# HGRN2 mix in three steps a group in place of six: levels in pairs, keys one step ahead, final transposes one group behind

## The chip, the cores and the metric

The kernel runs on one core of one Trainium2 chip. The metric is the device time of one execution in microseconds (us), and a kernel's time is the median of several executions. The engines, by the names that the profile uses, are PE (TensorE, with PEld for its weight loads), DVE (VectorE), ACT (ScalarE), POOL (GpSimd) and SP (SyncE, which issues the DMAs).

## The reference, cut to what matters

One step of a two-layer encoder: 1,024 prompt frames and eight streams of 16 frames, so nine chunks of 128 rows. Each layer multiplies the normalised frames by one input matrix, runs four kinds of recurrence (four heads or head pairs each) over the result, and multiplies by an output matrix. The change is in the fourth kind, HGRN2. Its recurrence has a decay for every channel:

```python
def hgrn_block(s_prev, xs):
    q, k, v, lf = xs
    b = jnp.cumsum(lf, axis=2)
    diff = b[:, :, :, None, :] - b[:, :, None, :, :]
    w = jnp.exp(jnp.where(causal_tril(l)[:, :, None], diff, -jnp.inf))
    s = jnp.einsum("bhtk,bhsk,bhtsk->bhts", q, k, w)
    o = jnp.einsum("bhts,bhsv->bhtv", s, v) + jnp.einsum("bhtk,bhkv->bhtv", q * jnp.exp(b), s_prev)
    s_new = jnp.exp(bl)[..., None] * s_prev + jnp.einsum("bhsk,bhsv->bhkv", k * jnp.exp(bl[:, :, None, :] - b), v)
    return s_new, o
...
    ho = head_rms(from_blocks(ho)) * h_norm_w.astype(f32).reshape(H_HEADS, H_HD)
    out_h = ho.reshape(bsz, t, GROUP_WIDTH) * jax.nn.silu(hg)
```

## The kernel before

**Units.** A layer is ten units in a fixed order: h0, r0, s0, m0, h1, r1, s1, m1, h2, h3 (h is an HGRN2 head, r retention, s Mamba-2, m mLSTM). A unit has a projection, which is most of PE's work, and a mix, its recurrence. `merge` (L1754 to 1782) writes both into one stream for each engine: the mix of one unit goes between the projection matmuls of the next. So the mixes of h0 and h1 lie in the projections of r0 and r1, that of h2 in h3's, and that of h3 in the first half of the output projection; in two layers there are eight HGRN2 mixes.

**The projection.** It works in fp32r as three products, hi by hi, lo by hi and hi by lo. In a token-major run ("tm", L425 to L427, 256 columns wide) and in a feature-major run ("fm", L404 to L406, 384 wide) it yields after every three matmuls. r0 and r1 have 216 yields, h3 has 120 (72 tm, then 48 fm), the first half of the output projection has 288.

**Steps.** A mix is a generator. After projection yield i, `merge` runs mix steps as long as j * yields * pace < i * steps, j being the steps already run. `steps` is a number that the unit gives. The pace is 1, but 0.9 from h2 to h3, where besides the last six steps of h2 are carried into the merge behind h3. What a step hands to `after(1, ...)` is issued at the start of the next step, ahead of that step's own work. All engines run in order, so this text order is the order in each queue, and every tile of PSUM comes from one ring of eight banks.

**One HGRN2 mix.** The nine chunks are three groups of three. The causal product with per-channel decay is cut into a base of 32x32 blocks and five levels (li = 0 to 4, blocks of 64, 32, 16, 8 and 4). For each group there are:

- `level` (L1486): two subtractions on DVE and an exp on ACT; a step later one multiply on POOL and one on DVE, all 192 columns wide.
- `prep` (L1505): decayed queries Q and keys K (exp on ACT, subtract on DVE), a step later the multiplies, K's on DVE and Q's on POOL.
- `base` (L1526): 12 matmuls of 32x32 (L1534).
- `pick` (L1540): the score blocks of one level, three matmuls of 64x64 or six of 32x32 (L1564), 12 of 32x16 (L1552); copies a step later, and after level 4 `diag` (L1574), four copies on DVE.
- `keys` (L1580): K transposed on PE (L1584). `state` (L1596): K transposed times values on PE (L1603), then `update` (L1613) on DVE. `out` (L1635): scores times values, queries times state (L1642, L1644).
- `post` (L1648): squares on ACT and the root mean square; a step later `scale` (L1662) on DVE. `fin` (L1667): three transposes on PE (L1671), evacuated on ACT.

The part of the step loop that sets the order (L1689 to 1716): a group takes six steps, li = -1 (base and prep) and li = 0 to 4 (a pick each). Each step also begins the level three picks ahead (LOOK = 3). At li = 4 that is level 2 of the next group, and at li = -1 of the next group it is level 2 again; the second overwrites the first. Around the six steps, keys are at li = 1, the state at li = 3, and of the group before, the outputs are at li = 0 and 1, post at 2 and fin at 4.

**What else DVE, ACT and POOL do there.** They split the weights into hi and lo, evacuate the projection, and for h3's fm run a forget-gate chain for each group (`ev_qf`, L1402: L526, L1415, L1417, L1424, then `fours`, L1435). In the output projection ACT and DVE split the mix read back from memory (mxh, mxl).

Of the kernel before, what the change touches and what calls it, by code (L numbers as in the profile page):

```python
# [51 lines left out]
NG = 3  # L52
CLAMP = -43.0
NLEV = 5
# [66 lines left out]
class Kernel:  # L121
# [1276 lines left out]
    def unit_h(self, l, h):  # L1398
# [52 lines left out]
        if h == 0:  # L1451
            gt = self.p_lay.tile([128, NCH, 16], F32, name="gt")
# [22 lines left out]
        def mix():  # L1475
            hw = self.vB[:, 40 + 4 * l + h:40 + 4 * l + h + 1]
            stt = {}
            LOOK = 3
# [6 lines left out]

            def level(W, g, li):  # L1486
                hs = 64 >> li
                w = G3 if (g < 2 or hs <= 8) else 256
                X = self.f()
                W["X"][li] = X, w  # L1490
                xv = lambda a: a[:, 0:w].rearrange("p (n e t) -> p n e t", e=2, t=hs)
                ref = xv(b[g])[:, :, 0, hs - 1:hs].to_broadcast([128, w // (2 * hs), hs])
                self.tt(xv(X)[:, :, 0], ref, xv(b[g])[:, :, 0], ALU.subtract)
                self.tt(xv(X)[:, :, 1], xv(b[g])[:, :, 1], ref, ALU.subtract)
                self.act(X[:, 0:w], X[:, 0:w], AF.Exp)

                def mults():
                    self.tt(xv(X)[:, :, 0], xv(X)[:, :, 0], xv(k[g])[:, :, 0], ALU.mult, "p")
                    self.tt(xv(X)[:, :, 1], xv(X)[:, :, 1], xv(q[g])[:, :, 1], ALU.mult)

                self.after(1, mults)

            sv = lambda a, n=3: a[:, 0:128 * n].rearrange("p (c t) -> p c t", t=128)

            def prep(g, W):  # L1505

                Q = self.f()
                K = self.f()
                np_ = 3 if g < 2 else 2
                e = bl.pop(g)  # L1510
                W.update(Q=Q, K=K, eL=e)
                self.act(Q, b[g], AF.Exp)
                self.tt(sv(K, np_), e[:, 0:np_][:, :, None].to_broadcast([128, np_, 128]), sv(b[g], np_), ALU.subtract)
                if g == 2:
                    s8 = lambda a: a[:, 256:384].rearrange("p (n t) -> p n t", t=16)
                    self.tt(s8(K), e[:, 2:10][:, :, None].to_broadcast([128, 8, 16]), s8(b[g]), ALU.subtract)
                self.act(K, K, AF.Exp)
                self.act(e[:, 0:3 if g < 2 else 10], e[:, 0:3 if g < 2 else 10], AF.Exp)

                def mults():  # L1520
                    self.tt(K, K, k[g], ALU.mult)
                    self.tt(Q, Q, q[g], ALU.mult, "p")

                self.after(1, mults)

            def base(g, W):  # L1526


                sc = self.ps("sc")
                for c in range(3):  # L1530
                    for j in range(4):
                        rs = slice(32 * j, 32 * j + 32)
                        ts = slice(128 * c + 32 * j, 128 * c + 32 * j + 32)
                        nc.tensor.matmul(sc[rs, 32 * c:32 * c + 32], k[g][:, ts], q[g][:, ts], start=True, stop=True)  # L1534
                W["ST"], W["D"] = ST, D = self.f(), self.t(96)
                nc.gpsimd.memset(ST, 0.0)
                nc.gpsimd.memset(D, 0.0)
                self.after(1, lambda: nc.vector.copy_predicated(D, self.lev[:, LEVW - 96:], sc[:, 0:96]))

            def pick(g, W, li):  # L1540
                hs = 64 >> li
                x, w = W["X"].pop(li)
                n = w // 128
                sc = self.ps("sc")
                half = lambda a: a.rearrange("p (n e t) -> p n e t", e=2, t=hs)[:, :, 1]
                if li >= 2:
                    D = W["D"]
                    for c in range(n):
                        for j in range(4):
                            rs = slice(32 * j, 32 * j + 32)  # L1550
                            xt = x[:, 128 * c + 32 * j:128 * c + 32 * j + 32]
                            nc.tensor.matmul(sc[rs, 16 * c:16 * c + 16].rearrange("p (n t) -> p n t", t=hs), xt, half(xt),  # L1552
                                             start=True, stop=True)
                    cp = lambda a: a.rearrange("p (n t) -> p n t", t=hs)
                    mk = self.lev[:, 48 * (li - 2):48 * (li - 2) + 16 * n]
                    self.after(1, lambda: nc.vector.copy_predicated(half(D[:, 0:32 * n]), cp(mk), cp(sc[:, 0:16 * n])))
                    if li == NLEV - 1:
                        self.after(1, lambda: diag(W))
                    return
                for c in range(n):  # L1560
                    for j in range(64 // hs):
                        rs = slice(64 * j, 64 * j + hs)
                        xt = x[:, 128 * c + 64 * j:128 * c + 64 * j + 2 * hs]
                        nc.tensor.matmul(sc[rs, hs * c:hs * c + hs], xt[:, 0:hs], xt[:, hs:2 * hs], start=True, stop=True)  # L1564

                def put():
                    for j in range(64 // hs):
                        rs = slice(64 * j, 64 * j + hs)
                        self.copy(sv(W["ST"][rs], n)[:, :, 64 * j + hs:64 * j + 2 * hs],
                                  sc[rs, 0:hs * n].rearrange("p (c t) -> p c t", t=hs), BIG[li])  # L1570

                self.after(1, put)
# [23 lines left out]
            def state(g, W):  # L1596

                n = 3 if g < 2 else 2
                tr = self.ps("tr")
                for cc in range(n):  # L1600
                    j, i = divmod(3 * g + cc, 2)
                    cs = slice(128 * cc, 128 * cc + 128)
                    nc.tensor.matmul(tr[:, cs], W["KT"][:, cs], v[j][:, i, 0], start=True, stop=True)  # L1603
                S = self.f()

                def update():
                    for cc in range(n):
                        c = 3 * g + cc
                        cs = slice(128 * cc, 128 * cc + 128)
                        if c == 0:  # L1610
                            self.copy(S[:, cs], tr[:, cs], "v")
                        else:
                            nc.vector.scalar_tensor_tensor(out=S[:, cs], in0=SS[c], scalar=W["eL"][:, cc:cc + 1], in1=tr[:, cs],  # L1613
                                                           op0=ALU.mult, op1=ALU.add)
                        SS[c + 1] = S[:, cs]
                        if c == 7:
                            self.dma(T["o_p_h"][l, h], S[:, cs])

                self.after(1, update)

            def state_s(W, jj):
                tr = self.ps("tr")
# [57 lines left out]
            Ws = [{"X": {}} for _ in range(NG)]  # L1680
# [3 lines left out]
            level(Ws[0], 0, 0)  # L1684
            yield
            level(Ws[0], 0, 1)
            for _ in range(2 if h < 2 else 2):
                yield
            for g in range(NG):  # L1689
                W = Ws[g]  # L1690
                for li in range(-1, NLEV):
                    if li < 0:
                        base(g, W)
                        prep(g, W)
                    else:
                        pick(g, W, li)
                    if li + LOOK < NLEV:
                        level(W, g, li + LOOK)
                    elif g + 1 < NG:
                        level(Ws[g + 1], g + 1, li + LOOK - NLEV)  # L1700
                    if li == 1:
                        keys(g, W)
                    if li == 3:
                        state(g, W)
                        if g == 1:
                            load_states()
                    if g > 0:
                        V = Ws[g - 1]
                        for cc in {0: (0,), 1: (1, 2)}.get(li, ()):
                            out(g - 1, V, cc)  # L1710
                        if li == 2:
                            post(g - 1, V)
                        if li == 4:
                            fin(g - 1, V)
                            Ws[g - 1] = None
                    yield
            W = Ws[2]
            yield
            yield
            out(2, W, 0)  # L1720
            out(2, W, 1)
            out(2, W, 2)
            yield
            post(2, W)
            yield
            state_s(W, 0)
            yield
            state_s(W, 1)
# [2 lines left out]
            fin(2, W)  # L1731
            yield

        return dict(runs=[("tm", ev_vg), ("fm", ev_qf)], mix=mix, steps=31 if h < 2 else 29, gate=(lambda: self.gate_prep(l, gt)) if h == 0 else None)


    def mix_load(self, l, half, g):
# [263 lines left out]
```

## Time and profile before

| | before |
|---|---|
| median of 3 runs | 2383.02 us (2382.79 to 2383.59) |
| profiled execution, device time | 2383.27 us |
| its span in the profile | 2381.4 us |
| PE busy in the span | 2315.6 us (97%) |
| DVE, ACT, POOL busy | 1367.5, 1082.4, 935.8 us |
| mean granted clock of PE | 0.994 of full |

The profile is that of one execution. PE is busy for all but 65.8 us of the span. The busy share of an engine is a mean over all stages; how engines stand to each other in an HGRN2 mix is seen only in a stretch that holds one. In the timeline a row merges neighbouring instructions of a line, under the shape of the first, and a matmul of fp32 values is recorded as two passes, so 12 instructions of 32x16 stand as x24.

### The profile page before, as it was taken

Reading aid. Unit: us, or ns where it says so; the run is one execution under the profiler, and the core shown is the slowest. Engines: PE = TensorE matmul, PEld = TensorE weight load, DVE = VectorE, ACT = ScalarE, POOL = GpSimd, SP = SyncE. Lnnn points to the kernel's source line nnn. Section 1 sums busy time; section 2 is a strip of 40 time slices with the busy share of each in tenths; the row PEclk is TensorE's granted clock in tenths of the full one; section 3 lists DMA queues with packets and bytes.
Section 4 is the critical chain, followed back from the end, with each engine's and each line's share of the span. In section 5 each row is a group of like instructions: output and inputs, shape, how many; then the busy total and the mean of one; then the engine's idle time right before and its main releaser. Section 6 shows DMA issues by size and latency. Waiting matters only on the chain.

```text
span 2381.4 us, 51682 instructions
## 1 busy us (share of the span) xinstructions
PE 2315.6 (97%) x20104; PEld 2251.8 (95%) x20104; DVE 1367.5 (57%) x3426; ACT 1082.4 (45%) x2881; POOL 935.8 (39%) x1117
## 2 busy tenths in 40 slices
PE   7999999999999998999999999999999999899998
PEld 7899999999999998999998999999899999888998
DVE  4756753774765377553258476537747555766532
ACT  6344563433555345424354445634344653453333
POOL 2442344353334335434316333433633452344341
PEclk9999999999999999999999999999999999999999
DMA  5111232221123222546411212322111323225462
GB/s 153 37 47 53 79 90 78 66 61 53 50 84 96 62 73 66 171 126 207 136 49 34 62 55 85 87 70 74 49 54 52 105 72 83 50 86 163 146 189 96
DMA packets 280048, 205.24 MB, mean 86 GB/s; under 512 B 56788, under 2 KB 272236, under 8 KB 279804
## 3 DMA queue, kind: packets, MB, share of 16 engines
q1 hardware_dynamic: 279484, 201.85, 29.9%
q8 instruction: 159, 2.61, 0.5%
q14 instruction: 85, 0.70, 0.1%
q0 software_dynamic: 320, 0.09, 0.0%
HBM read 149.58 MB, written 52.29 MB: 85 GB/s over the span
## 4 chain that ended last, share of the span: by engine, by line
PE 84%; DVE 8%; ACT 4%; DMA 1%; issue 1%; SPq 1%; POOL 1%; ACTq 0%; DVEq 0%; POOLq 0%
PE w L425 16%; PE w L427 16%; PE w L426 16%; PE w L404 6%; PE w L405 6%; PE w L406 6%; DVE f L212 3%; ACT f L215 2%; PE w L1289 1%; DVE c L212 1%; DMA c<-mixd 1%; PE w L1642 1%; PE w L1603 1%; PE w L1552 1%; PE w L1043 1%
## 5 line engine op out<-in xcount | busy, mean ns | idle before, releaser
L425 PE MATMUL w<-hi,hnh 128*128 128x256 f32 (+1 forms) x2592 | 773.3, 298 | 0.0
L427 PE MATMUL w<-hi,hnl 128*128 128x256 f32 (+1 forms) x2592 | 730.1, 282 | 1.6 <-DVE hnl L492 1.4
L426 PE MATMUL w<-lo,hnh 128*128 128x256 f32 (+1 forms) x2592 | 729.3, 281 | 0.0
L425 PEld LDWEIGHTS w<-hi,hnh 128*128 128x128 f32 x2592 | 490.6, 189 | 5.7 <-issue 0.8
L426 PEld LDWEIGHTS w<-lo,hnh 128*128 128x128 f32 x2592 | 490.9, 189 | 2.9
L427 PEld LDWEIGHTS w<-hi,hnl 128*128 128x128 f32 x2592 | 490.3, 189 | 2.2 <-DVE hnl L492 2.0
L215 ACT ACTIVATE f<-f 128x384 f32<-128x384 f32 (+1 forms) x460 | 236.3, 516 | 427.7 <-DVE f L212 263.5
L215 ACT ACTIVATE c<-c 128x512 f32<-128x512 f32 (+3 forms) x398 | 211.3, 534 | 286.3 <-DVE c L526 202.2
L212 POOL TENSOR_TENSOR f<-f,f 128x384 f32<-128x384 f32 (+2 forms) x268 | 225.6, 849 | 290.7 <-ACT f L215 216.3
L404 PE MATMUL w<-hnh,hi 128*128 128x384 f32 x960 | 338.8, 353 | 0.0
L425 PE MATMUL w<-hi,mxh 128*128 128x256 f32 x1152 | 329.4, 286 | 0.0
L427 PE MATMUL w<-hi,mxl 128*128 128x256 f32 x1152 | 325.2, 282 | 0.2 <-POOL mxl L212 0.2
L426 PE MATMUL w<-lo,mxh 128*128 128x256 f32 x1152 | 324.9, 282 | 0.0
L406 PE MATMUL w<-hnh,lo 128*128 128x384 f32 x960 | 324.6, 338 | 0.0
L405 PE MATMUL w<-hnl,hi 128*128 128x384 f32 x960 | 324.6, 338 | 0.0
L212 POOL TENSOR_TENSOR lo<-raw,hi 128x512 fp32r<-128x512 f32 x148 | 196.4, 1327 | 304.3 <-ACT hi L202 278.3
L212 POOL TENSOR_TENSOR c<-c,c 128x512 f32<-128x512 f32 (+2 forms) x144 | 160.3, 1122 | 273.3 <-ACT c L215 169.5
L425 PEld LDWEIGHTS w<-hi,mxh 128*128 128x128 f32 x1152 | 219.0, 190 | 1.4 <-issue 0.6
L427 PEld LDWEIGHTS w<-hi,mxl 128*128 128x128 f32 x1152 | 219.0, 190 | 0.8 <-POOL mxl L212 0.8
L426 PEld LDWEIGHTS w<-lo,mxh 128*128 128x128 f32 x1152 | 218.2, 189 | 0.0
L212 DVE TENSOR_TENSOR lo<-raw,hi 128x512 fp32r<-128x512 f32 x140 | 114.8, 820 | 149.9 <-ACT hi L202 149.7
L404 PEld LDWEIGHTS w<-hnh,hi 128*128 128x128 f32 x960 | 181.5, 189 | 3.0 <-issue 1.8
(295 smaller groups left out, 3876.8 us busy)
## 6 DMA issues: line engine op xcount, KB each, us to landing
raw<-in_w_in SPq DMA_DIRECT2D x224, 128.0 KB
raw<-in_w_in SPq DMA_DIRECT2D x112, 256.0 KB
c<-mixd SPq DMA_DIRECT2D x96, 192.0 KB
raw<-in_w_out SPq DMA_DIRECT2D x64, 256.0 KB
mixd<-c SPq DMA_DIRECT2D x48, 256.0 KB
xd<-c SPq DMA_DIRECT2D x48, 256.0 KB
c<-xd SPq DMA_DIRECT2D x48, 256.0 KB
c<-sscr SPq DMA_DIRECT2D x36, 256.0 KB
```

Of the source, the lines that this page charges most:

```text
L212: (self.nc.vector if e == "v" else self.nc.gpsimd).tensor_tensor(out=out, in0=a, in1=b, op=op)
L215: self.nc.scalar.activation(out=out, in_=in_, func=func, scale=scale, bias=bias, **k)
L404: nc.tensor.matmul(o, hi[:, k, ms], xhi[:, k, :], start=(k == 0), stop=False)
L405: nc.tensor.matmul(o, hi[:, k, ms], xlo[:, k, :], start=False, stop=False)
L406: nc.tensor.matmul(o, lo[:, k, ms], xhi[:, k, :], start=False, stop=(k == KT - 1))
L425: nc.tensor.matmul(o, xhi[:, k, ts], hi[:, k, :w], start=(k == 0), stop=False)
L426: nc.tensor.matmul(o, xhi[:, k, ts], lo[:, k, :w], start=False, stop=False)
L427: nc.tensor.matmul(o, xlo[:, k, ts], hi[:, k, :w], start=False, stop=(k == KT - 1))
L1043: nc.tensor.matmul(po[h], w[:, h], v[j][:, i, h], start=(c in (0, 8)), stop=(c < 8))
L1289: nc.tensor.matmul(po[:, 64 * h:64 * h + 64], pt[:, h], x_[:, 64 * h:64 * h + 64], start=True, stop=True)
L1552: nc.tensor.matmul(sc[rs, 16 * c:16 * c + 16].rearrange("p (n t) -> p n t", t=hs), xt, half(xt), start=True, stop=True)
L1603: nc.tensor.matmul(tr[:, cs], W["KT"][:, cs], v[j][:, i, 0], start=True, stop=True)
```

## The change

The group loop is written out with three steps, called A, B and C here:

- A: base, pick 0, levels 3 and 4 begun, the state of the group before, post of the group two before.
- B: picks 1 and 2, keys, level 0 of the next group begun.
- C: picks 3 and 4, the three outputs of the group before, fin of the group two before, levels 1 and 2 and prep of the next group begun (in the last group, the loads of the streams' states instead).

Each level, and with prep the decayed keys and queries, is begun two steps ahead of the matmul that takes it. Level 2 of a next group is begun once. The state's update is issued in the same step as its matmuls, not a step later. The prelude begins three levels and prep; the tail brings the last state, post and fin. `steps` goes from 31 to 21 (h0, h1) and from 29 to 19 (h2, h3).

```diff
@@ state
-                self.after(1, update)
+                update()
@@ mix, the group loop
-            for _ in range(2 if h < 2 else 2):
+            level(Ws[0], 0, 2)
+            prep(0, Ws[0])
+            yield
+            yield
+            for g in range(NG):
+                W, V = Ws[g], Ws[g - 1]
+                base(g, W)
+                pick(g, W, 0)
+                level(W, g, 3)
+                level(W, g, 4)
+                if g > 0:
+                    state(g - 1, V)
+                if g > 1:
+                    post(g - 2, Ws[g - 2])
                 yield
-            for g in range(NG):
-                W = Ws[g]
-                for li in range(-1, NLEV):
-                    if li < 0:
-                        base(g, W)
-                        prep(g, W)
-                    else:
-                        pick(g, W, li)
-                    if li + LOOK < NLEV:
-                        level(W, g, li + LOOK)
-                    elif g + 1 < NG:
-                        level(Ws[g + 1], g + 1, li + LOOK - NLEV)
...
+                pick(g, W, 1)
+                pick(g, W, 2)
+                keys(g, W)
+                if g + 1 < NG:
+                    level(Ws[g + 1], g + 1, 0)
+                yield
+                pick(g, W, 3)
+                pick(g, W, 4)
+                if g > 0:
+                    for cc in range(3):
+                        out(g - 1, V, cc)
+                if g > 1:
+                    fin(g - 2, Ws[g - 2])
+                if g + 1 < NG:
+                    level(Ws[g + 1], g + 1, 1)
+                    level(Ws[g + 1], g + 1, 2)
+                    prep(g + 1, Ws[g + 1])
+                else:
+                    load_states()
+                yield
             W = Ws[2]
...
+            state(2, W)
+            post(1, Ws[1])
+            yield
+            yield
+            for cc in range(3):
+                out(2, W, cc)
             yield
             post(2, W)
-            yield
+            fin(1, Ws[1])
             state_s(W, 0)
             yield
             state_s(W, 1)
@@
-        return dict(runs=[("tm", ev_vg), ("fm", ev_qf)], mix=mix, steps=31 if h < 2 else 29, gate=(lambda: self.gate_prep(l, gt)) if h == 0 else None)
+        return dict(runs=[("tm", ev_vg), ("fm", ev_qf)], mix=mix, steps=21 if h < 2 else 19, gate=(lambda: self.gate_prep(l, gt)) if h == 0 else None)
```

The order on PE in group 1 of h1, before: pick 1 between two projection matmuls, with the keys' transposes and two outputs of group 0 (w is a PSUM tile, f and c are tiles in SBUF, hi and lo weights, hnh and hnl the input).

```order
3285 L427 MATMUL w_6577<-hi_6088,hnl_159 128x256
3286 L1564 MATMUL w_6590<-f_6395 32x32 x6
3287 L1584 MATMUL w_6601<-cst,f_6512 128x128 x3
3288 L1642 MATMUL w_6561<-c_5182,f_6210 128x128
3289 L1644 MATMUL w_6561<-f_6403,f_6214 128x128
3290 L1642 MATMUL w_6561<-c_5302,f_6210 128x128
3291 L1644 MATMUL w_6561<-f_6403,f_6214 128x128
3292 L425 MATMUL w_6577<-hi_6088,hnh_158 128x256
```

Of the change, step B of the same group.

```order
3289 L427 MATMUL w_6560<-hi_6076,hnl_159 128x256
3290 L1564 MATMUL w_6582<-f_6444 32x32 x6
3291 L1552 MATMUL w_6589<-f_6448 32x16 x12
3292 L1584 MATMUL w_6602<-cst,f_6453 128x128 x3
3293 L425 MATMUL w_6560<-hi_6076,hnh_158 128x256
```

Pick 2, which stood 21 projection matmuls later, now follows pick 1 directly, and the outputs have gone to step C. Counted over the program, 176 stretches of HGRN2 matmuls stand between projection matmuls before and 112 now; those with score blocks (bases and picks) are 144 before and 72 now, of which 24 hold a base and a pick 0, and 48 two picks.

The order on DVE before, at the state of group 1 of h1: a copy of pick 3 and half of a level, then `update` (L1613), issued a step after its matmuls.

```order
703 L212 TENSOR_TENSOR f_6707<-f_6026 128x4x32 x2
704 L1556 COPY_PREDICATED t_6508<-lev,w_6694 128x6x8
705 L212 TENSOR_TENSOR f_6707<-f_6707,f_5999 128x4x32
706 L1613 SCALAR_TENSOR_TENSOR f_6715<-f_6403,bl_5947,w_6711 128x128
707 L1613 SCALAR_TENSOR_TENSOR f_6715<-f_6715,bl_5947,w_6711 128x128 x2
```

Of the change, steps A (to the second L1613 row) and the start of B, in group 1 of h1.

```order
679 L205 COPY f_6280<-t_6281 32x3x32 x4
680 L212 TENSOR_TENSOR f_6444<-f_6444,f_5819 128x6x32
681 L212 TENSOR_TENSOR f_6448<-f_6448,f_5819 128x12x16
682 L212 TENSOR_TENSOR f_6453<-f_6453,f_5925 128x384
683 L212 TENSOR_TENSOR f_6521<-f_5923 128x24x8 x2
684 L212 TENSOR_TENSOR f_6525<-f_5923 128x48x4 x2
685 L205 COPY f_6533<-w_6529 128x128
686 L1613 SCALAR_TENSOR_TENSOR f_6533<-f_6533,bl_5746,w_6529 128x128 x2
687 L1538 COPY_PREDICATED t_6514<-lev,w_6500 128x96
688 L205 COPY f_6513<-w_6517 64x3x64
689 L212 TENSOR_TENSOR f_6521<-f_6521,f_5819 128x24x8
690 L212 TENSOR_TENSOR f_6525<-f_6525,f_5819 128x48x4
```

The multiplies for levels 1 and 2 and the keys, four subtractions and the update of group 0 (685, 686) now stand in one step, the update ahead of the multiplies (689, 690) that picks 3 and 4 of step C take.

## Rows read from the trace of the kernel before

**Rows 1.** Page, part 1: busy us, share of the span and instructions of each engine

```profile
PE 2315.6 (97%) x20104; PEld 2251.8 (95%) x20104; DVE 1367.5 (57%) x3426; ACT 1082.4 (45%) x2881; POOL 935.8 (39%) x1117
```

**Rows 2.** Waits of PE: line and what it waited for, us in total, times, longest

```profile
PE w L1671 <- DVE f L1662: 12.5, 4, 4.1
PE w L1584 <- DVE f L212: 12.0, 8, 2.9
PE w L1564 <- POOL f L212: 6.9, 4, 3.2
PE w L1603 <- ACT f L202: 4.4, 7, 0.7
PE w L1552 <- POOL f L212: 4.3, 5, 1.2
```

**Rows 3.** Windows of 3.4 us: busy us of each engine (instructions), granted clock, DMA

```profile
513.50:516.90 3.40, 3.40 (x17) 3.40 (x18) 2.87 (x9) 1.05 (x2) 0.77 (x1) 0.51 0.02 5
2162.20:2165.60 3.40, 3.31 (x15) 3.16 (x16) 1.49 (x5) 0.58 (x1) 3.40 (x4) 0.50 0.72 231
```

**Rows 4.** Timeline of PE round one pick: start, us, instruction, [idle before]

```profile
111.42 0.28 PE L426 MATMUL w<-lo,hnh 128*128 128x256 f32 x1
111.54 0.28 PE L427 MATMUL w<-hi,hnl 128*128 128x256 f32 x1
111.75 0.38 PE L1552 MATMUL w<-f 128*32 128x16 f32 x24
112.06 0.38 PE L425 MATMUL w<-hi,hnh 128*128 128x256 f32 x1
112.28 0.28 PE L426 MATMUL w<-lo,hnh 128*128 128x256 f32 x1
```

**Rows 5.** Groups of PE by line and shape: count, busy us, mean ns, idle before

```profile
L1552 PE MATMUL w<-f 128*32 128x16 f32 x1664 | 27.1, 187 | 4.4 <-POOL f L212 4.3
```

**Rows 6.** Timeline, GpSimd then PE, at level 0 of group 0 (h2 mix)

```profile
889.87 2.74 POOL L212 TENSOR_TENSOR f<-f,f 128x384 f32<-128x384 f32 x3 [1.73 <-ACT f L215]
892.66 0.56 PE L1564 MATMUL w<-f 128*64 128x64 f32 x6 [1.97 <-POOL f L212]
```

**Rows 7.** Timeline, DVE then PE, at the key transposes of unit h0

```profile
107.23 2.51 DVE L212 TENSOR_TENSOR f<-f,f 128x384 f32<-128x384 f32 x2
108.81 0.41 PE L1584 MATMUL w<-cst,f 128*128 128x128 f32 x2 [2.41 <-DVE f L212]
```

**Rows 8.** Timeline, DVE then PE, at the final transposes beside a forget-gate chain

```profile
945.30 0.86 DVE L1662 SCALAR_TENSOR_TENSOR f<-w,s,c 128x128 f32<-128x128 f32 x3
945.79 0.75 PE L1671 MATMUL w<-cst,f 128*128 128x128 f32 x3 [2.24 <-DVE f L1662]
```

**Rows 9.** Timeline, PE, DVE, PE: outputs and final transposes in the output projection

```profile
961.90 0.39 PE L1642 MATMUL w<-c,f 128*128 128x128 f32 x2
975.30 0.36 DVE L1448 TENSOR_SCALAR f<-t 128x384 f32<-128x384 f32 x1
982.84 0.85 DVE L1662 SCALAR_TENSOR_TENSOR f<-w,s,c 128x128 f32<-128x128 f32 x3
983.23 0.85 PE L1671 MATMUL w<-cst,f 128*128 128x128 f32 x3 [3.02 <-DVE f L1662]
```

**Rows 10.** Groups of DVE by line and shape: count, busy us, mean ns, idle before

```profile
L212 DVE TENSOR_TENSOR f<-f 128x192 f32<-128x192 f32 x208 | 114.6, 590 | 0.0
L212 DVE TENSOR_TENSOR f<-f,f 128x192 f32<-128x192 f32 x104 | 51.9, 499 | 21.1 <-ACT f L215 20.7
L212 DVE TENSOR_TENSOR f<-f,f 128x384 f32<-128x384 f32 x24 | 16.8, 698 | 0.0
L205 DVE COPY f<-t 32x96 f32<-32x96 f32 x96 | 23.5, 244 | 1.8
L1613 DVE SCALAR_TENSOR_TENSOR f<-f,bl,w 128x128 f32<-128x128 f32 x56 | 19.4, 346 | 3.3 <-PE w L1603 1.9
```

**Rows 11.** Windows, columns as in group 3, of a mix stretch of unit h0

```profile
113.50:129.00 15.50, 14.25 (x180) 13.09 (x179) 14.51 (x39) 6.09 (x17) 9.37 (x15) 1.00 0.09 20
```

More of the change, by code (lines that the diff above doesn't have):

```diff
@@ L1686, in mix @@
             level(Ws[0], 0, 1)
-            for _ in range(2 if h < 2 else 2):
-                yield
-            for g in range(NG):
-                W = Ws[g]
-                for li in range(-1, NLEV):
-                    if li < 0:
-                        base(g, W)
-                        prep(g, W)
-                    else:
-                        pick(g, W, li)
-                    if li + LOOK < NLEV:
-                        level(W, g, li + LOOK)
-                    elif g + 1 < NG:
-                        level(Ws[g + 1], g + 1, li + LOOK - NLEV)
[L1701 to L1716, printed above, removed]
@@ L1717, in mix @@
-            W = Ws[2]
+            level(Ws[0], 0, 2)
+            prep(0, Ws[0])
             yield
             yield
-            out(2, W, 0)
-            out(2, W, 1)
-            out(2, W, 2)
+            for g in range(NG):
[29 more added lines that the diff above has]
+                yield
@@ L1723, in mix @@
+            W = Ws[2]
+            state(2, W)
[4 more added lines that the diff above has]
+                out(2, W, cc)
             yield
             post(2, W)
-            yield
+            fin(1, Ws[1])
             state_s(W, 0)
```

## The prediction

> **What bounds the kernel now.** I read the page's first part, the waits of PE, the windows of low granted clock, then the timeline at each kind of wait. PE bounds the whole: busy 2315.6 us, and no other engine has two thirds of that [rows 1]. So an edit in the mix is worth what it takes from PE's stream, its waits, or its time at the low clock. The waits that belong to HGRN2 are five kinds, 12.5 + 12.0 + 6.9 + 4.4 + 4.3 = 40.1 us [rows 2]: the final transposes wait for the scale (L1662), the key transposes for the multiply on DVE, the picks for the multiply on POOL, the state matmuls for the evacuated keys. Each is an operand begun one or two short steps before PE takes it. Besides, seven stretches of 3.4 us stand at half the granted clock, 1.2 in place of 2.4 GHz; the first and the last are shown [rows 3], and the last begins as a wait of 4.1 us for the scale ends [rows 2, 3].
>
> The sum below is made against the profiled execution, 2383.27 us, which lies 0.25 us above the median of 2383.02.
>
> **The change part by part.**
>
> *Fewer entries into the array.* Projection matmuls start 0.12 us apart; from the last one ahead of a pick to the second one behind it are 111.54 to 112.28 = 0.74 us, where two spacings would be 0.24 [rows 4]. The extra is 0.50. The pick's merged row is 0.38 long and one pass in it 0.187 [rows 4, 5], so the 24 passes take 0.38 - 0.19 = 0.19 from first start to last, and the remaining 0.31 is entering and leaving. Two picks behind each other should pay that once. There are 72 stretches with score blocks fewer: 48 are two picks on 32 rows, 48 * 0.31 = 14.9 us. The other 24 pair a base on 32-row tiles with a 64x64 pick, which no row shows; I take half, 24 * 0.155 = 3.7. Together **18.6 us**. Bounds: 0 (each block drains by itself) to 72 * 0.31 = 22.3; no loss, as the same matmuls run between the same neighbours.
>
> The pick in rows 4 shows that going between a projection matmul and a 32-row pick costs 0.31 us. The Trainium skill, TensorEngine Tiling (Array Packing), Key Properties, says: "Mode switching requires drain: Changing tiling mode (not just tile) drains the TensorE." The row agrees; by the rule the pair of base and 64x64 pick would drain between its halves too and save nothing, the sum of this part would be 14.9, and no run here shows such a pair.
>
> *The waits that go.* The key multiply and the levels now start a longer and earlier step ahead. A step of h0 and h1 is 216/21 = 10.3 yields of three matmuls, 10.3 * 0.36 = 3.7 us of projection, where it was 216/31 = 7.0 and 2.5; and keys and levels now have one full step between their multiplies' issue and the matmul. The wait of 2.41 us was for DVE's pair of multiplies of 2.51 us issued in the step just ahead [rows 7], the one of 1.97 for three on POOL, 2.74 us [rows 6]. At the same durations 3.7 us and the mix on top cover both. The 12.0 and 6.9 and 4.3 us go almost wholly, as do the 4.4 at the state matmuls, since keys are evacuated a step or more before.
>
> *The final transposes.* In h2 they stand beside h3's forget-gate chains. Group 0's (two waits, 2.24 us in the one shown [rows 8]) get their scale a step earlier and lie a whole chain later: gone. The other two, the larger ones, I expect to stay. Of group 1, post is now the last step ahead of the output projection, so the scale is issued in its first step, on DVE right behind the third forget-gate chain. That chain's last instruction starts at 975.30 and is 0.36 long, and the scale's first third takes some 0.34 [rows 9, 10], so operands are there at about 976.0. PE begins the output projection at 961.9 [rows 9] and comes to the transposes 24 yields later, 24 * 0.36 + 0.9 for the outputs ahead = 9.5 us: 971.4. So PE would wait **about 5 us** in each of the two layers, 10 us, where it waited for group 2's scale (3.02 [rows 9], the other 4.1). Group 2's transposes stand at yield 58, past all that.
>
> *The waits that come.* `update` is now issued in the step of its own matmuls, ahead of levels 3 and 4's multiplies on DVE. What is queued behind it are these multiplies, the base's copy and pick 0's. Step A has on DVE: four diagonal copies 0.98, two level multiplies 1.00, the keys' multiply 0.70, four subtractions 2.36, three updates 1.04, in all 6.1 us [rows 10], against some 4.7 of PE (3.7 and about 1.0 of base, pick and state). So DVE reaches the update last, some 5 us after the step's start, when PE's state matmuls are past: it doesn't wait for PE. But it ends step A 1.4 us late. Step B has two multiplies 1.00, two subtractions 1.18 and a scale of three, some 1.0; step C a multiply 0.50, four subtractions 2.36 and the keys' 0.70; with small copies about 3.8 each [rows 10], against 4.7 and more of PE, so the lateness is made up within a group. In group 2 the keys' PSUM bank is released by that update; I allow 0.6 us in each of eight mixes, 5 us. For the denser h2, 2 us in each layer, 4 us.
>
> Left of the 40.1 us are 10 + 5 + 4 = 19; **21 us** go. Bounds: 33 (only 7 left) and 5 (35 left).
>
> *The low clock.* A stretch of 3.4 us at half costs 1.7 us. I expect the two behind the output projection's wait to stay and one elsewhere: seven become three, 4 * 1.7 = **6.8 us**; bounds 2 and 10.
>
> *Work taken off other engines.* The second issue of level 2 goes: 16 levels of two subtractions and a multiply on DVE, 16 * (2 * 0.59 + 0.50) = 26.9 us [rows 10], with an exp on ACT and a multiply on POOL. None of it is on PE; it is what lets DVE carry shorter groups, and I count it at nothing itself.
>
> *Moved with them.* The two loads of the streams' states go from group 1 to the last step of group 2, behind the mix fetches on SP's queue. They have two steps of 3.7 us before the outputs take them in h0 and h1. I count nothing; were they late by one step, 3.7 * 8 = 30 us would come back, part of the rivals below.
>
> Sum: 2383.3 - 18.6 - 21 - 6.8 = **2337 us**. With all good ends 2383.3 - 22.3 - 33 - 10 = 2318, with all bad ones 2383.3 - 0 - 5 - 2 = 2376; together in one direction they are unlikely, and I take 2314 to 2362 as the main case's own range.
>
> **The rivals.**
>
> *DVE becomes the bound of the groups.* Before, a stretch of h0's mix had DVE busy 14.51 of 15.50 us [rows 11]. A group now has about 6.1 + 3.8 + 3.8 = 13.7 us on DVE, in three steps of 4.7 to 5.4 us of PE, some 14.8; other work on DVE (clamps, splitting weights) is not in that. For it: no slack to speak of. Against it: the duplicate level is gone, and the prelude has begun three levels ahead. If the lateness of step A (1.4, with small copies 1.8 us) comes out on PE in groups 1 and 2 of eight mixes, 16 * 1.8 = 29 us: 2366.
>
> *The update stops DVE: slower.* If PE is late into step A, DVE stands at L1613 until the state matmuls have run, with the multiplies for picks 3 and 4 behind it, and PE then stands at those picks. The chain from update to pick is 1.04 + 1.00 + copies and the POOL half, about 3.5 us; in 24 groups 84 us, so 2337 + 84 = 2421. It makes the change slower than before from 46/24 = 1.9 us a group on. Against it: pick and multiply are a step of 3.7 us apart, and before DVE waited 1.9 us in all for L1603 [rows 10].
>
> *Nothing comes of it.* Each block drains by itself and the waits only move: 2383 - 5 = 2378 at the least saving, within reach of 2383.
>
> *The pairs of unlike tiles drain.* Then the 3.7 us of base and pick 0 don't come: 2341. Rows 4 shows a drain where the whole array meets 32-row tiles, which speaks for it as much as against.
>
> **How the numbers follow.** Main case with either end for the unlike pairs 0.73 (of which 0.3 is the 2341 variant, inside its range); DVE as the bound 0.15; update slower 0.07; nothing 0.05. About 0.2% (4.8 us) is what a measurement of this kernel can tell from no change. Faster: 0.73 + 0.15 = 0.88; same 0.05; slower 0.07. The range reaches from the main case's low end to DVE's rival at 2366, and leaves out the last two cases and the main case's tails.
>
> **What would show it.** PE's waits at the key transposes and picks should fall from 23.2 us to a few; the four waits at the final transposes should be two, of some 5 us, early in the output projection, each with a low-clock stretch behind it. A pair of picks should take, from the last projection matmul ahead to the second behind, 0.74 + 0.19 = 0.93 us. DVE's wait for L1603 should stay under a few us. The prediction is wrong if a pair takes 1.24, if PE waits at picks 3 and 4 in each group, or if DVE is busy throughout the groups with PE waiting at each key transpose.

## The result and the profile after

The changed kernel takes 2366.02 us (median of four runs, 2365.48 to 2368.27) against 2382.90 of before (four runs): a ratio of 0.9932, 95% interval 0.9915 to 0.9949. It is faster by 17 us where 46 were forecast, and its time lies at the very end of the range, where the rival with DVE as the bound stood and not the main case.

| | before | after |
|---|---|---|
| profiled execution, device time | 2383.27 us | 2365.53 us |
| its span | 2381.4 | 2363.8 |
| PE busy | 2315.6 | 2299.2 |
| span less PE busy | 65.8 | 64.6 |
| waits of PE at HGRN2's lines | 40.1 (five kinds; 1.1 more at the outputs) | 38.6 |
| time at half the granted clock, the end left out | 23.9 in 7 stretches | 34.1 in 6 |

So nearly all of the 17.6 us of span came out of PE's busy time (16.4), and the waits stayed in sum. The page's first part and the waits of PE after the change:

```profile
PE 2299.2 (97%) x20104; PEld 2247.7 (95%) x20104; DVE 1340.5 (57%) x3378; ACT 1075.9 (46%) x2865; POOL 922.5 (39%) x1101
```

```profile
PE w L1564 <- POOL f L212: 17.7, 9, 3.1
PE w L1671 <- DVE f L1662: 13.4, 2, 7.1
...
PE w L1552 <- DVE f L212: 4.1, 4, 1.7
...
PE w L1552 <- POOL f L212: 1.8, 5, 0.7
...
PE w L1584 <- DVE f L212: 1.6, 2, 0.8
```

Beside [rows 2]: the key transposes (L1584) fell from 12.0 to 1.6 us, and the state matmuls (L1603, 4.4) are gone from the list. The picks of levels 0 and 1 (L1564) rose from 6.9 to 17.7, and the final transposes (L1671) have two waits in place of four, with more in them. DVE has 48 instructions fewer, those of level 2, and 27 us less of busy time.

**The entries.** Two picks behind each other, and a base with a pick 0 (timeline of PE after: start, us, instruction):

```profile
1011.84 0.28 PE L427 MATMUL w<-hi,mxl 128*128 128x256 f32 x1
1012.05 0.60 PE L1552 MATMUL w<-f 128*32 128x16 f32 x48
1012.58 0.38 PE L425 MATMUL w<-hi,mxh 128*128 128x256 f32 x1
```

```profile
105.67 0.28 PE L427 MATMUL w<-hi,hnl 128*128 128x256 f32 x1
105.88 0.40 PE L1534 MATMUL w<-f,f 128*32 128x32 f32 x24
106.21 0.56 PE L1564 MATMUL w<-f 128*64 128x64 f32 x6
...
106.92 0.28 PE L426 MATMUL w<-lo,hnh 128*128 128x256 f32 x1
```

From the last projection matmul to the first behind it a pair of picks takes 0.74 us, where one pick took 0.52 [rows 4]: 0.22 us more for a whole second pick, whose extra alone was 0.50. The pair saves some 0.28; to the second projection matmul, at 1012.80, it takes 0.96 us, where 0.93 was forecast. A base and a pick 0 take 1.25 us to the second projection matmul, 1.01 over two spacings of 0.12; before, a base alone cost 0.75 - 0.24 = 0.51 in the same way (0.52 is the median of 24), and a 64x64 pick alone 0.92 - 0.24 = 0.68 (timeline of PE before):

```profile
98.80 0.28 PE L427 MATMUL w<-hi,hnl 128*128 128x256 f32 x1
99.01 0.40 PE L1534 MATMUL w<-f,f 128*32 128x32 f32 x24
...
99.55 0.28 PE L426 MATMUL w<-lo,hnh 128*128 128x256 f32 x1
```

```profile
500.89 0.28 PE L427 MATMUL w<-hi,hnl 128*128 128x256 f32 x1
501.10 0.56 PE L1564 MATMUL w<-f 128*64 128x64 f32 x6
...
501.81 0.28 PE L426 MATMUL w<-lo,hnh 128*128 128x256 f32 x1
```

So this pair saves 0.19 (0.52 + 0.68 - 1.01).

**The final transposes in the output projection.** ACT, DVE and PE in layer 1, after the change:

```profile
958.73 2.61 ACT L202 ACTIVATE mxh<-c 128x384 fp32r<-128x384 f32 x5 [1.89 <-DMA c<-mixd]
960.31 2.28 DVE L212 TENSOR_TENSOR mxl<-c,mxh 128x384 fp32r<-128x384 f32 x2 [0.46 <-ACT mxh L202]
962.51 0.55 DVE L526 TENSOR_SCALAR f<-w 128x384 f32<-128x384 f32 x1
...
968.87 0.36 DVE L1448 TENSOR_SCALAR f<-t 128x384 f32<-128x384 f32 x1
969.14 0.86 DVE L1662 SCALAR_TENSOR_TENSOR f<-w,s,c 128x128 f32<-128x128 f32 x3
969.54 0.99 PE L1671 MATMUL w<-cst,f 128*128 128x128 f32 x3 [7.05 <-DVE f L1662]
```

The scale starts as the third forget-gate chain ends (968.87 + 0.36), as forecast, and PE has been waiting since 962.49. The chain begins at L526, 10.7 us after the output projection's first matmul (951.78); before, it began 7.3 us after it (961.54):

```profile
968.85 0.55 DVE L526 TENSOR_SCALAR f<-w 128x384 f32<-128x384 f32 x1
```

The windows of low clock that begin inside this wait, and inside its sibling in layer 2 (columns as in rows 3):

```profile
965.66:972.49 6.83, 2.95 (x14) 2.80 (x15) 5.67 (x13) 3.46 (x8) 4.20 (x6) 0.50 0.38 119
2133.02:2143.26 10.24, 5.97 (x28) 5.82 (x29) 6.99 (x14) 5.89 (x13) 7.17 (x8) 0.50 0.37 115
```

PE was idle for about half of either (busy 2.95 of 6.83 and 5.97 of 10.24 us), so these cost well under half their length.

**Level 0 on POOL.** DVE, ACT, POOL and PE in the first mix, group 1 (the multiply of level 0 is the first of the three in the second POOL row):

```profile
118.63 0.61 DVE L212 TENSOR_TENSOR f<-f 128x192 f32<-128x192 f32 x2
119.33 0.53 ACT L215 ACTIVATE f<-f 128x384 f32<-128x384 f32 x1 [1.18 <-DVE f L212]
120.52 1.56 POOL L212 TENSOR_TENSOR c<-c,c 128x256 f32<-128x256 f32 x2 [3.04 <-DVE c L212]
...
124.91 2.00 POOL L212 TENSOR_TENSOR f<-f,f 128x192 f32<-128x192 f32 x3
125.87 0.83 PE L1564 MATMUL w<-f 128*64 128x64 f32 x6 [2.08 <-POOL f L212]
```

The exp is done at 119.86. POOL comes to the multiply at 124.91, five us later: ahead of it stand the retention unit's rotary products, which had themselves waited 3.04 us for DVE's evacuation. Four of the nine waits at L1564 look like this one, 8.4 us together, all at the 64x64 pick in r0 and r1; a fifth wait at that pick, 1.3 us, is in h3. The largest of the rest, 3.1 and 2.8 us, are at pick 1 of h2's group 0, in h3; there POOL's multiply stands behind a weight split and a gate product.

By units, as the time from one unit's first projection matmul to the next unit's, read from the trace (us; the last column is a version that the experiments led to):

| | before | after | late transposes and level 0 on DVE |
|---|---|---|---|
| r0, layers 1 and 2 | 101.33, 102.22 | 101.50, 100.75 | 97.68, 99.08 |
| r1 | 99.63, 99.35 | 96.99, 96.97 | 94.15, 94.87 |
| h3 | 78.27, 80.37 | 70.37, 72.11 | 70.01, 71.78 |
| output projection, first half | 130.14, 131.19 | 131.89, 133.62 | 127.19, 129.41 |

A row holds one HGRN2 mix, so some 2.3 us of saved entries (18.0 over eight mixes) are in each figure of the two later columns. h3 gained 16 us in both layers together, 8.4 of it waits of PE; r0 and the output projection, where the waits grew, gained 1.5 us at most or lost.

### The profile page after: what moved, and what is told of

Same layout as the page of the kernel before. It is cut to its first block, busy times and chain, and to the rows that moved or that the text cites. A ratio compares the mean times of both kernels' runs of the same rounds, so it can differ in the third digit from the quotient of the medians.

```text
span 2363.8 us, 51602 instructions
## 1 busy us (share of the span) xinstructions
PE 2299.2 (97%) x20104; PEld 2247.7 (95%) x20104; DVE 1340.5 (57%) x3378; ACT 1075.9 (46%) x2865; POOL 922.5 (39%) x1101
## 4 chain that ended last, share of the span: by engine, by line
PE 82%; DVE 8%; ACT 3%; POOL 2%; DMA 2%; issue 1%; SPq 1%; ACTq 0%; POOLq 0%; DVEq 0%
PE w L427 16%; PE w L425 16%; PE w L426 15%; PE w L404 6%; PE w L406 6%; PE w L405 6%; DVE f L212 2%; ACT f L215 2%; DMA c<-mixd 2%; POOL c L212 1%; PE w L1289 1%; DVE c L212 1%; PE w L1642 1%; PE w L489 1%; PE w L1043 1%
## 5 line engine op out<-in xcount | busy, mean ns | idle before, releaser
L427 PE MATMUL w<-hi,hnl 128*128 128x256 f32 (+1 forms) x2592 | 731.0, 282 | 1.5 <-DVE hnl L492 1.4
L427 PEld LDWEIGHTS w<-hi,hnl 128*128 128x128 f32 x2592 | 491.1, 189 | 2.1 <-DVE hnl L492 1.9
L215 ACT ACTIVATE f<-f 128x384 f32<-128x384 f32 (+1 forms) x444 | 224.2, 517 | 378.1 <-DVE f L212 193.9
L427 PE MATMUL w<-hi,mxl 128*128 128x256 f32 x1152 | 324.9, 282 | 1.0 <-POOL mxl L212 1.0
L212 POOL TENSOR_TENSOR f<-f,f 128x384 f32<-128x384 f32 (+2 forms) x252 | 212.4, 859 | 232.7 <-ACT f L215 168.8
L427 PEld LDWEIGHTS w<-hi,mxl 128*128 128x128 f32 x1152 | 218.7, 190 | 1.5 <-POOL mxl L212 1.4
L212 DVE TENSOR_TENSOR lo<-raw,hi 128x512 fp32r<-128x512 f32 x140 | 122.0, 871 | 151.6 <-ACT hi L202 151.4
L212 DVE TENSOR_TENSOR c<-c,w 128x512 f32<-128x512 f32 (+1 forms) x112 | 74.2, 665 | 199.3 <-PE w L427 158.0
```

The lines of the kernel that those rows point to most:

```text
L212: (self.nc.vector if e == "v" else self.nc.gpsimd).tensor_tensor(out=out, in0=a, in1=b, op=op)
L215: self.nc.scalar.activation(out=out, in_=in_, func=func, scale=scale, bias=bias, **k)
L427: nc.tensor.matmul(o, xlo[:, k, ts], hi[:, k, :w], start=False, stop=(k == KT - 1))
```

## The experiments

Each is the changed kernel with one edit, if nothing else is said. Ratios are against the kernel before, measured on the same chip; the changed kernel stands at 0.9932. Gains in us are differences of medians, within 2 us of what the ratios give; the intervals of two ratios together leave about 5 us to either side of such a difference.

**Blocks apart.** Each step is cut in halves, and base, pick 2 and pick 4 stand in the second half; `after` lags, `steps` and the steps carried behind h3 are doubled.

```diff
-                base(g, W)
                 pick(g, W, 0)
                 level(W, g, 3)
...
                 yield
+                base(g, W)
+                yield
                 pick(g, W, 1)
-                pick(g, W, 2)
                 keys(g, W)
...
                 yield
+                pick(g, W, 2)
+                yield
                 pick(g, W, 3)
-                pick(g, W, 4)
...
                 yield
+                pick(g, W, 4)
+                yield
```

> The changed kernel with each step cut in two halves: the first pick and all else in the first half, the second block (base, pick 2, pick 4) in the second, so a base and a pick, or two picks, no longer stand behind each other on PE; what was issued one step later is issued two halves later. Theory (each of 72 stretches costs an entry of 0.31 us more, 0.19 for the base and pick 0): 48 * 0.29 + 24 * 0.19 = 18 us more, 2384. Rival (entries cost nothing, and the 17 us gained came from waits): 2366 within 4.

Measured 2382.39 us, ratio 0.9996 (0.9986 to 1.0005): 16.4 us of the change's 17 are given back, near the 18 expected. PE's busy time is 15.7 us more than the changed kernel's 2299.2, and its idle time, 65.1 us, is the same within 0.5; the waits hardly moved (L1564 18.0 us, L1671 12.3).

```profile
PE 2314.9 (97%) x20104; PEld 2252.1 (95%) x20104; DVE 1339.3 (56%) x3378; ACT 1076.4 (45%) x2865; POOL 922.3 (39%) x1101
```

In the same way as above, as medians at the full clock and without a wait, a base alone takes 0.76 us here and a 64x64 pick 0.92; together they took 1.25 in the changed kernel, so with the two spacings (0.24) taken off once, 0.19 is saved again. Pick 1 with the keys takes 1.03 and pick 2 alone 0.74, and together they took 1.20: 0.33 saved. The gain that the change made is that of the entries.

**Transposes later.** In h2's mix `fin(1)` moves behind the streams' second state.

```diff
             post(2, W)
-            fin(1, Ws[1])
+            if h != 2:
+                fin(1, Ws[1])
             state_s(W, 0)
             yield
             state_s(W, 1)
             yield
+            if h == 2:
+                fin(1, Ws[1])
             yield
```

> Of the changed kernel (2366 us) one thing is moved: in h2's mix alone the final transposes of group 1 stand two steps later, in the step after the streams' second state. Theory (the saved entries came as forecast, and the gain was lost where PE waits at those transposes behind the third forget-gate chain, 7.05 and 6.36 us, and in the low clock that follows): the two waits go, 13.4 us, and part of the low-clock time beside them (6.8 and 10.2 us at half, worth up to 5), so 2348 to 2353 us. Rival (the forget-gate chain holds PE anyway, through group 2's transposes or the output projection's operands): the wait reappears a few us later at another line, and the time stays at 2363 to 2367.

Measured 2357.85 us, 0.9891 (0.9875 to 0.9908): 8 us gained, between theory and rival. The waits at L1671 are gone, but 5.6 us of new waits stand at the projection's own operand (PE w L427 for mxl on POOL, 1.0 to 6.6 us). PE and POOL there, layer 1:

```profile
967.58 0.38 PE L427 MATMUL w<-hi,mxl 128*128 128x256 f32 x1 [2.14 <-POOL mxl L212]
```

```profile
965.73 0.75 POOL L209 COPY bl<-f 128x2 f32<-128x2 f32 x2 [4.38 <-DVE f L1424]
966.44 1.09 POOL L212 TENSOR_TENSOR mxl<-c,mxh 128x384 fp32r<-128x384 f32 x1
```

POOL's split of the mix stands behind a tiny copy that waits for the same forget-gate chain. So the chain holds PE on a second way, and of 13.4 us of waits about 8 could be had; PE's idle time fell by 7.9 us, from 64.6 to 56.7.

**Level 0 on DVE.** One word in `level`:

```diff
-                    self.tt(xv(X)[:, :, 0], xv(X)[:, :, 0], xv(k[g])[:, :, 0], ALU.mult, "p")
+                    self.tt(xv(X)[:, :, 0], xv(X)[:, :, 0], xv(k[g])[:, :, 0], ALU.mult, "v" if li == 0 else "p")
```

> Of the changed kernel, level 0's first multiply (half of the columns) is done on DVE in place of POOL; 24 multiplies of about 0.5 us change engines. Theory (PE waits for level 0's pick, five of nine waits and about 8 of 17.7 us at L1564, because that multiply stands on POOL behind the retention unit's rotary products, which wait for DVE's evacuation): the waits at the 64x64 pick of groups 1 and 2 go, 6 to 9 us, 2357 to 2361. Rival (DVE itself is late in these steps, as it was forecast for DVE as the bound): adding 0.5 us to DVE per group lengthens the same waits, 2366 to 2375.

Measured 2357.74 us, 0.9892 (0.9877 to 0.9907): 8 us gained, as the theory had it, with more work on DVE (1345.8 us busy after 1340.5). Waits of PE:

```profile
PE w L1671 <- DVE f L1662: 14.4, 2, 7.4
...
PE w L1564 <- POOL f L212: 7.9, 4, 3.0
```

L1564 fell from 17.7 to 7.9 us (0.9 more stands under DVE), all waits at the picks from 23.6 to 15.3, and r0 and r1 became 1.7 to 3.3 us shorter in each layer. The cause of these waits was POOL's queue, not DVE.

**Update a step later.**

```diff
-                update()
+                self.after(1, update)
```

> Of the changed kernel, the state's update is issued a step after its matmuls again, as before the change. DVE now waits 23.3 us at the update for PE's state matmuls. Theory (that wait is an effect, PE stands at level 0's pick ahead of the state matmuls, and DVE has time): within 3 us of 2366. Rival (the update at the head of DVE's queue keeps the multiplies for picks 3 and 4 from running, and so causes PE's waits): 2366 less 5 to 15 us.

Measured 2373.78 us, 0.9962 (0.9947 to 0.9977): 8 us slower, which neither expected. The units r0, r1 and h3 moved by 0.7 us in all (single ones by up to 1.6 either way); the output projections lost 5.4 and 4.3. There, DVE and PE:

```profile
965.14 0.36 DVE L1448 TENSOR_SCALAR f<-t 128x384 f32<-128x384 f32 x1
965.41 0.72 DVE L1613 SCALAR_TENSOR_TENSOR f<-f,bl,w 128x128 f32<-128x128 f32 x2
```

```profile
965.81 0.79 PE L1644 MATMUL w<-f,f 128*128 128x128 f32 x2 [11.94 <-DVE f L1613]
```

The last state's update falls behind the third forget-gate chain, and the outputs wait 12 us for it (12.8 in layer 2), in place of the 7.1 and 6.4 us at the final transposes. The immediate update is what keeps it ahead of that chain.

**Update a step later in the groups only** (`update() if g == 2 else self.after(1, update)`).

> The changed kernel with the state's update a step after its matmuls in groups 0 and 1, and in the same step only for group 2 (the tail). The kernel with all updates a step later lost 8 us in the output projection alone, where the last update came behind the third forget-gate chain and PE waited 12 us for it in each layer. Theory (in the groups the place of the update decides nothing, in the tail it is worth those 8 us and more): 2364 to 2368. Rival (the update at the head of DVE's queue causes PE's waits in the groups): 2355 to 2362.

Measured 2363.92 us, 0.9917 (0.9901 to 0.9934): just between the two forecasts, and not to be told from the changed kernel. The interval alone would leave room for a gain of some us; the trace shows none in the waits: PE waits 23.3 us at the picks (23.6 in the changed kernel) and is idle for 65.0 us (64.6). DVE's wait for the state matmuls, in the changed kernel

```profile
DVE f L1613 <- PE w L1603: 23.3, 6, 5.0
```

stays at 19.6 us in four waits of 4.9. All four are at the update of group 2 in r0 and r1, the tail, where no wait of PE stands. So the update at the head of DVE's queue does no harm that shows.

**Level 2 begun twice again.** In step B, beside `level(Ws[g + 1], g + 1, 0)`, a `level(Ws[g + 1], g + 1, 2)` whose result is overwritten.

> The changed kernel with level 2 of the next group begun in step B as well as in step C, the first overwritten by the second: the work that the change took off comes back, 16 * 1.7 = 27 us on DVE, 16 exps and 16 multiplies on POOL, none of it awaited by PE. Theory (PE waits where an operand is behind particular instructions on POOL or DVE; DVE has room elsewhere): level 0's multiply on POOL, next to it, is delayed by up to 0.7 us in groups 1 and 2, 16 * 0.2 to 0.5 = 3 to 8 us more, 2369 to 2374. Rival (DVE's throughput bounds the groups): most of the 27 us appear, 2383 to 2393.

Measured 2366.69 us, 0.9927 (0.9913 to 0.9942): no change. The page's first part shows the load put back, DVE 1340.5 to 1362.2 us and POOL 922.5 to 939.2. PE's waits at the picks are shorter at L1564 and longer at L1552, in all 24.4 us where they were 23.6.

```profile
PE 2295.7 (97%) x20104; PEld 2244.1 (95%) x20104; DVE 1362.2 (58%) x3426; ACT 1082.0 (46%) x2881; POOL 939.2 (40%) x1117
```

```profile
PE w L1564 <- POOL f L212: 15.9, 9, 2.8
...
PE w L1552 <- POOL f L212: 5.6, 10, 1.3
PE w L1552 <- DVE f L212: 2.9, 5, 1.7
```

DVE's throughput doesn't bound the groups. The theory's 3 to 8 us don't show either, though the interval doesn't rule out their lower end.

**The kernel before with level 2 begun once** (the one issued at li = 4 left out).

> The kernel before with level 2 of a next group begun once (the first of the two issues left out): 27 us less on DVE, 16 exps and multiplies fewer, the steps as they were. Theory (worth nothing by itself, PE's waits there are for other multiplies): 2380 to 2384. Rival (a lighter DVE and POOL is a good part of the change's 17 us): 2370 to 2378.

Measured 2381.22 us, 0.9991 (0.9982 to 1.0000): some 2 us, and by the interval 4 at most. That part of the change is worth little alone.

**Both edits**: transposes later and level 0 on DVE.

> The changed kernel with both edits: h2's final transposes of group 1 two steps later, and level 0's first multiply on DVE. Theory (the two waits are independent, one in r's projections, one in the output projection): the gains of 8.2 and 8.3 us add, 2349 to 2351. Rival (both draw on the same DVE time or the same low-clock stretches): 2353 to 2358.

Measured 2345.23 us, 0.9843 (0.9828 to 0.9857): 21 us under the changed kernel and 37 under the kernel before, so the two gains add, as the theory had it: they are 8 and 8 us by the medians and 9.8 and 9.5 by the ratios, and 21 agrees with either sum within the intervals (2345 lies 4 us under the theory's range). PE's idle time is 47.1 us, 17.5 less than in the changed kernel. It is the fastest version of the study. Its waits of PE:

```profile
PE w L1564 <- POOL f L212: 7.9, 4, 3.0
PE w L427 <- POOL mxl L212: 5.0, 4, 2.1
```

**Both edits, and levels 1 and 2 of h2's group 0 on DVE** (`"v" if li == 0 or (h == 2 and g == 0 and li < 3) else "p"`).

> As the kernel with both edits, and in h2's group 0 levels 1 and 2 have their first multiply on DVE as well (four multiplies in all). Theory (PE waits about 3 us in each layer at group 0's pick 1 because POOL's multiplies stand behind a gate product and a weight split): these two waits go, 4 to 6 us less than without, 2344 to 2347. Rival (DVE, busy with the same levels, is no sooner): within 2 us of the kernel with both edits.

Measured 2348.28 us, 0.9856 (0.9840 to 0.9873): nothing gained; PE's idle time in h3 is 10.4 us in the two layers, where it was 10.2. In h3, layer 1, the wait at pick 1 shrank from 3.02 to 1.07 us, with 0.53 at the keys, and a new one of 3.17 us came a step later, at the picks of levels 3 and 4, again for POOL (level 3's multiply behind a gate product that waits for ACT):

```profile
898.12 1.08 PE L1552 MATMUL w<-f 128*32 128x16 f32 x40 [3.17 <-POOL f L212]
```

```profile
896.80 0.72 POOL L212 TENSOR_TENSOR c<-c,t 128x256 f32<-128x256 f32 x1 [3.92 <-ACT c L215]
```

**Both edits, and h3's gate product on DVE.**

```diff
-                    self.tt(s, s, z, ALU.mult, "p")
+                    self.tt(s, s, z, ALU.mult, "v" if h == 3 else "p")
```

> The kernel with both edits (late transposes in h2, level 0's first multiply on DVE), and in h3's token-major run the gate product (128x256) is done on DVE in place of POOL. PE waits 3 us in each layer at group 0's pick 1 for POOL, whose three multiplies come behind a weight split and that gate product, which waits for ACT. Theory (POOL's queue ahead of the multiplies is the cause): about 1.5 us go in each layer, with others of its kind 3 to 5 us, 2340 to 2343. Rival (the weight split ahead, or DVE, which gets the product, holds the same picks): within 2 us of 2345.

Measured 2347.18 us, 0.9851 (0.9837 to 0.9866): the rival. The gate product waits for ACT on DVE as it did on POOL, and DVE's own halves of the levels stand behind it:

```profile
889.72 0.64 DVE L212 TENSOR_TENSOR c<-c,t 128x256 f32<-128x256 f32 x1 [1.38 <-ACT c L215]
890.29 1.88 DVE L212 TENSOR_TENSOR f<-f,f 128x192 f32<-128x192 f32 x3
```

PE's wait at pick 1 is 3.0 us still: POOL has its half of pick 1 done at 889.53, but DVE's half ends at 891.43, and PE goes on at 891.58. What would take h3's 4 to 6 us of waits a layer away stays open; to put ACT's part of the gate elsewhere wasn't tried.

## Why the prediction was wrong

**Entries (18.6 us): right.** 0.31 and 0.155 us a pair were forecast, 0.28 and 0.19 measured, 48 * 0.28 + 24 * 0.19 = 18.0; PE's busy time fell by 16.4 and the blocks apart gave 16.4 back. The Trainium skill, TensorEngine Tiling (Array Packing), Key Properties, has a drain at every change of the tiling mode. A base and a 64x64 pick that stand apart change it four times, in and out of each, and behind each other three times; so by that rule the pair saves one change of four, and not nothing, as the prediction and its rival of 2341 us read it. The rows agree with the rule so counted: half of 0.31 is 0.155, and 0.19 was measured.

**The waits that go (21 us net): this step failed.** 40.1 became 38.6. At the key transposes and picks, where 23.2 us should have fallen to a few, they are 25.2.

- Keys and states: right, 16.4 us to 1.6. Key multiplies begun a step ahead are off PE's way.
- "The 12.0 and 6.9 and 4.3 us go almost wholly" was wrong for the last two: picks went from 11.2 to 23.6 us. I set the step's 3.7 us against the multiply's own duration (0.7 to 2.7 us on POOL) and didn't count what stands ahead of it on POOL. There, in the row above, it came to its turn five us after its operand, behind another unit's products. The same row that I read, a wait for POOL, doesn't tell how long POOL had been at other work. The edit that moved the multiply gave 8 us. At picks 3 and 4 PE waited for DVE four times, 4.1 us in all, each time in group 0, where no update stands ahead.
- The final transposes: the mechanism, the place and the count were right (two waits, behind the third chain), and the term was too small, 10 us against 13.4. I put the operands at 976.0, 14.5 us after the output projection's first matmul (961.54), as before the change; they came 17.7 us after it (951.8 to 969.5), since the chain began 3.4 us later: ahead of it on DVE stand splits of the mix, for which ACT waited on a load. PE came 10.7 us after the first matmul, where 9.9 was forecast.
- The update's bank and h2's denser steps, 9 us allowed: no wait for that bank shows; the two waits at the keys, 0.8 us each, are for DVE's multiply. In h3 PE is idle for 4.1 and 6.8 us in the two layers (3.1 and 5.2 of it at the picks), less than before by 8 us in all.
- The moved loads of the streams' states: nothing, as counted; no wait of PE for them shows.

**The low clock (6.8 us): wrong in sign.** 23.9 us at half the clock became 34.1, and the two longest stretches begin inside the two waits at the final transposes, which grew. But much of their length lies in PE's idle time: PE was busy for 23.7 us at half the clock before and 25.1 after, which at half speed costs an estimated 11.8 and 12.6 us, 0.7 more.

So the sum: 18.0 of 18.6, 1.5 of 21, and -0.7 of 6.8 give 18.8 us where the profiled executions differ by 17.7.

**The rivals.** DVE as the bound named 2366, and the time agrees to the microsecond, but by luck: 22 us put back on DVE changed nothing, and one of the edits that took 8 us off the time put more work on DVE. The update that stops DVE: DVE did wait for the state matmuls, 23.3 us where under a few were forecast, but 19.8 of them in the tails of r0 and r1, and none of it reached PE. In the tail of h2, at the start of the output projection, the opposite was true: there the late update makes PE wait 12 to 13 us a layer in place of 6 to 7. The base and pick 0 saved 0.19 us of the 0.31 that a pair on 32 rows was to save.

## What to carry to other kernels

A wait for an operand that another engine makes is sized by what stands ahead of the producer in its queue, not by the producer: follow the queue back to the first instruction that waits, before a step is made shorter or moved. When small matmuls are gathered behind each other, the entry into the array that is saved is a term that can be read from one row and holds: here 18.6 us were forecast for it and 16.4 given back. A long chain on a shared engine should have nothing behind it in text that PE takes soon; look at which instruction is issued just behind each such chain, since one step's difference made PE wait 12 to 13 us a layer here in place of 6 to 7, and cost 8 us of time.

## What the runs showed of the hardware

The mean of 0.59 us for DVE's subtractions [rows 10] is a mixture. In the version with both edits four of them ran in 1.15 us while POOL was idle, and in the changed kernel four of the same form took 3.07 while POOL was at its products:

```profile
883.30 1.15 DVE L212 TENSOR_TENSOR f<-f 128x192 f32<-128x192 f32 x4
```

```profile
881.07 2.10 POOL L212 TENSOR_TENSOR f<-f,f 128x384 f32<-128x384 f32 x2 [1.73 <-ACT f L215]
886.87 1.28 POOL L212 TENSOR_TENSOR lo<-raw,hi 128x512 fp32r<-128x512 f32 x1 [3.71 <-ACT hi L202]
```

```profile
121.40 3.07 DVE L212 TENSOR_TENSOR f<-f 128x192 f32<-128x192 f32 x4
```

```profile
121.40:124.47 3.07, 2.39 (x42) 2.14 (x40) 3.07 (x6) 0.52 (x1) 2.91 (x5) 1.00 0.00 0
```

That is 0.29 against 0.77 us for one; in the second stretch POOL was busy for 2.91 of 3.07 us (the window's columns are those of rows 3). Counted over the changed kernel, 98 of these 192 subtractions overlap no instruction of POOL and took 0.34 to 0.36 us each; 70 lie over 90% beside POOL's work and took 0.90 in the mean, from 0.34 to 1.45. So POOL's work goes with longer instructions on DVE, and a sum of mean durations says little of a stretch in which both are busy. The Trainium skill, SBUF — State Buffer, "SBUF: two separate sides", says that DVE, for an instruction with two inputs in SBUF, and GpSimd share a port pair under an exclusive lock, which the one that comes second waits for; these subtractions have two such inputs. The rows agree in direction, and none of the runs took the two engines apart on purpose.
